# A two-layer hybrid decoder step on one core: inputs laid out on the host, a first stage by channel tiles, low weights and gate norms on VectorE, and new job ranks

## The chip, the cores and the metric

The kernel runs on one core of a Trainium2 chip as a single program. The metric is the device time of one execution in microseconds (us), as the median of several runs. PE is TensorE's matmul side and PEld its weight loads; DVE is VectorE, ACT ScalarE, POOL GpSimd, SP SyncE, from whose queue the kernel issues its DMAs.

## The reference

One inference step over a prompt of 1024 rows and 32 sample rows (8 sequences of 4), with 1024 channels and two layers. Each layer computes

```
x <- x + gate(c) * Branch(RMSNorm(x) * (1 + scale(c)) + shift(c)),   (shift, scale, gate) = silu(c) @ w_mod + b_mod
```

Layer 0 is sliding-window attention: 16 query heads on 4 key heads of 64 channels, a window of 128, a learned sink for each head, and for the samples a cache of 128 keys and values. Layer 1 is the gated DeltaNet: 8 query and key heads, 16 value heads of 128 channels, a causal convolution of length 4 ahead of q, k and v, and

```
S_t = e^{g_t} S_{t-1} + k_t u_t^T,   u_t = beta_t (v_t - (e^{g_t} S_{t-1})^T k_t),   o_t = S_t^T q_t / sqrt(128)
conv = silu(conv1d([conv_buf; h @ w_in][qkv]));   out = (rms_norm(o) * o_norm_g * silu(z)) @ w_out
```

The samples start from a state and a convolution buffer that are inputs. Outputs are y for both, the new keys and values, the new convolution buffers and the new states. Everything is float32.

## The kernel before, in words

All matrix products with weights are made of three products in a reduced form: both factors are split into a high and a low part (`wh`, `wl` for weights, `hhi`, `hlo` or `h2hi`, `h2lo` for activations), and high x high, high x low and low x high are summed in PSUM. The 1056 rows of both groups are handled as columns in three groups, `GRP`: 0 to 384, 384 to 768 and 768 to 1056. `project` takes, for one tile of 128 weight columns, 8 channel tiles x 3 products for each group, 72 products in all. `projector(plan)` runs a list of such tiles: `w_raw` loads raw weights two tiles ahead, and the job `ahead` splits the next tile's two halves when the counter `ticks`, one for each channel tile and group, has gone on by the two numbers of `SP`. `split_w` lets ACT cast the high part and POOL subtract it for the low part.

From the first attention projection on, the work around projections is written as generators. `weave(gen, name, hq)` puts one in a list of jobs by its rank (`K[name]`, or `KR[hq][name]` for a round's jobs), and after each product `stages()` goes through the list in order of rank and lets each job go on whose condition holds. The conditions (`ready`, `soon`, `idle`) look at engine-free times that the recording class `Core` adds up for each instruction as it is issued. So the ranks, `SP` and these times set one fixed order of instructions on each engine. Helpers issue through `Core`'s `Engine.call`, which is why nearly all instructions stand at one line of the kernel (L89).

The stages, with their times in the profiled execution:

- First stage, to 67 us. `scale_x` forms the row norms (twelve small DVE operations) and scales tiles of x in place; `turn_x` transposes them on PE, and ACT and DVE copy the results to `zo`. `modulation` multiplies silu(c) with halves of w_mod (products of 512 columns into one PSUM tile), `shape_h(0)` and `shape_h(1)` form hhi and hlo for four channel tiles each, and `first_half` makes the products for the first key and query tiles.
- Layer 0, to 415 us: the other projections, the attention of blocks, and `cached_pair`, which loads cached keys of two sequences and transposes them on PE. `modulation_rest` forms layer 1's modulation.
- The output projection of layer 0 and the shaping for layer 1, to 545 us.
- Layer 1, to about 1400 us: eight rounds, one for each key head, with six tiles of projection (q, k, two v, two z) as the stream between which jobs run. `conv` evacuates a projection into XR, convolves on DVE, and its job `samples` convolves the samples' columns on POOL with two PE transposes. `solve` and `invert` find the inverses of 64 triangular blocks of 32x32 on 64 partitions, by two DVE operations for each of 31 columns; `chain` runs through the eight chunks of 128 rows; `gating`, one job for each pair of chunks, norms the outputs (`rsqrt_pool`, on POOL) and multiplies with the gate.
- The output projection of layer 1 and the samples, to the end. `states_times` loads the samples' states and multiplies them with their keys and queries; `core` solves the samples' rule and updates the states.

Of the kernel before, what the change touches and what calls it, by code (L numbers as in the profile page):

```python
# [5 lines left out]
F32 = mybir.dt.float32  # L6
# [8 lines left out]
P = 128  # L15
# [16 lines left out]
def constants():  # L32
# [16 lines left out]
    blocks["lo32"] = (i[:, None] % 32 >= np.arange(32)[None, :]) * 1.0  # L49
# [9 lines left out]
    hsel = np.zeros((P, P))  # L59
    for kv in range(4):  # L60
        for r in range(32):
            hsel[kv * 4 + (r % 16) // 4, 32 * kv + r] = 1.0
    blocks["hsel"] = hsel
# [4 lines left out]
    order = ["ident", "iu", "ones", "mku", "lo32", "bsel", "fold32", "fold64", "wmask", "hsel", "smask", "selp", "sels"]  # L68
# [151 lines left out]
def body(tc, I, O, cst_ap, dbg=None):  # L220
    nc = tc.nc
    from contextlib import ExitStack, nullcontext
    es = ExitStack()
# [15 lines left out]
    SP = (2, 20)  # L239
    AM = (4, 8)  # L240
    K = dict(split=3, add=3, attend=12, turning=14, modulate=31, cached=9, wo=7, turn=0, ahead=6, taps=4, gating=5, decay=2, samples=28, load=5, mod=9, shape=9, decays=8, prepare=1, gather=11, finish=54, states=21, core=4, new=9)
    KR = [{'chain': 8, 'output': 9, 'solve': 5, 'invert': 21, 'blocks': 10, 'decayed': 0}, {'chain': 0, 'output': 3, 'solve': 12, 'invert': 10, 'blocks': 35, 'decayed': 35}, {'chain': 33, 'output': 2, 'solve': 22, 'invert': 19, 'blocks': 33, 'decayed': 34}, {'chain': 22, 'output': 12, 'solve': 3, 'invert': 4, 'blocks': 30, 'decayed': 17}, {'chain': 14, 'output': 0, 'solve': 1, 'invert': 17, 'blocks': 31, 'decayed': 57}, {'chain': 3, 'output': 13, 'solve': 6, 'invert': 20, 'blocks': 55, 'decayed': 29}, {'chain': 8, 'output': 1, 'solve': 11, 'invert': 20, 'blocks': 73, 'decayed': 34}, {'chain': 10, 'output': 8, 'solve': 4, 'invert': 28, 'blocks': 40, 'decayed': 44}]
# [10 lines left out]
    XB, FB, ZK, HK0, HK1 = 14, 3, 5, 7, 3  # L253
# [11 lines left out]
    gT = cp.tile([P, 2, KD], F32, name="gT")  # L265
    bT = cp.tile([P, 48], F32, name="bT")
# [9 lines left out]

    def xload(t):
        xt = xp.tile([P, D], F32, tag="xt", name="xt", bufs=XB)[0:P if t < NB else TS]
        nc.sync.dma_start(xt, xp_rows[t * P:(t + 1) * P] if t < NB else xs_rows)
        return xt  # L280

    def wmod_load(i):

        wms = []
        for k in range(KD):
# [2440 lines left out]
```

## Time and profile before

| | |
|---|---|
| time of the runs | 1695.62 us median of 3 (1692.66 to 1700.45) |
| profiled execution, span | 1699.2 us; the views give no other time for it |
| PE busy | 1613.3 us (95%) |
| PEld busy | 1417.4 us (83%) |
| DVE busy | 1207.9 us (71%) |
| ACT busy | 865.5 us (51%) |
| POOL busy | 581.8 us (34%) |
| granted clock, mean | 0.987 |
| DMA | 191.76 MB, 113 GB/s over the span |

A row of a table of stretches reads: stretch and length, busy time of each engine with the number of instructions, granted clock of PE, share of the DMA engines, GB/s. A row of a timeline reads: start, duration (of all its instructions), engine, line, operation, what it writes from what it reads, shapes, and in brackets the idle time ahead and who ended it. A group's row gives its busy time, the mean of one in ns, and the idle time ahead. A row of waits gives us in all, times and the longest.

### The profile page before, as it was taken

How to read it: one execution, taken by the hardware profiler on the slowest of the kernel's cores; microseconds unless marked ns; L12 is line 12 of the kernel's file. 1: busy time of each engine (PE TensorE's matmuls, PEld its weight loads, DVE VectorE, ACT ScalarE, POOL GpSimd, SP SyncE). 2: the span in 40 equal slices, each digit the busy share in tenths (PEclk: the TensorE clock that was granted, in tenths of full speed). 3: DMA queues.
4: the chain of work that ended last, by engine and by line, in shares of the span. 5: the costliest groups of instructions: out<-in, count | busy, mean ns of one | idle time of the engine just before them, and what ended most of it. 6: DMA issues, size and time to landing. Idle time of an engine off the chain costs nothing. (4 is left out here: it accounts for less than half of the span.)

```text
span 1699.2 us, 31431 instructions
## 1 busy us (share of the span) xinstructions
PE 1613.3 (95%) x10554; PEld 1417.4 (83%) x10554; DVE 1207.9 (71%) x3540; ACT 865.5 (51%) x2517; POOL 581.8 (34%) x1042
## 2 busy tenths in 40 slices
PE   6999999998999999999999999999999998989896
PEld 4988888986678899988989999899999996667784
DVE  5526676564665578878889788788788876367776
ACT  6625565443344565366463755655656654233332
POOL 2501111111222334363442644345344454333232
PEclk9999999998999999999999999999999999999998
DMA  9532121223343232132422324124241237855885
GB/s 345 158 123 73 53 59 48 59 81 93 116 136 105 79 77 65 59 99 73 118 56 69 89 66 129 46 79 111 54 124 49 55 97 225 245 165 169 243 259 166
DMA packets 281571, 191.76 MB, mean 113 GB/s; under 512 B 98361, under 2 KB 253881, under 8 KB 281378
## 3 DMA queue, kind: packets, MB, share of 16 engines
q1 hardware_dynamic: 281410, 189.75, 38.8%
q8 instruction: 84, 1.38, 0.4%
q14 instruction: 77, 0.63, 0.1%
HBM read 144.68 MB, written 47.04 MB: 113 GB/s over the span
## 5 line engine op out<-in xcount | busy, mean ns | idle before, releaser
L89 PE MATMUL ps_pj<-h2hi,wh 128*128 128x384 f32 (+1 forms) x1128 | 380.1, 337 | 0.0
L89 PE MATMUL ps_pj<-h2hi,wl 128*128 128x384 f32 (+1 forms) x1128 | 378.9, 336 | 0.6 <-POOL wl L89 0.5
L89 PE MATMUL ps_pj<-h2lo,wh 128*128 128x384 f32 (+1 forms) x1128 | 379.3, 336 | 0.0
L89 POOL TENSOR_TENSOR wl<-wr,wh 128x512 fp32r<-128x512 f32 x122 | 165.0, 1354 | 533.2 <-ACT wh L89 470.7
L89 PEld LDWEIGHTS ps_pj<-h2hi,wl 128*128 128x128 f32 x1128 | 213.5, 189 | 4.6 <-POOL wl L89 1.2
L89 PEld LDWEIGHTS ps_pj<-h2hi,wh 128*128 128x128 f32 x1128 | 213.5, 189 | 2.4
L89 PEld LDWEIGHTS ps_pj<-h2lo,wh 128*128 128x128 f32 x1128 | 213.2, 189 | 2.6
L89 POOL TENSOR_TENSOR xt<-xt,y 128x512 f32<-128x512 f32 (+1 forms) x48 | 63.6, 1329 | 174.3 <-DVE y L89 140.7
L89 PE MATMUL ps_pj<-hlo,wh 128*128 128x384 f32 (+1 forms) x360 | 119.6, 332 | 0.0
L89 PE MATMUL ps_pj<-hhi,wh 128*128 128x384 f32 (+1 forms) x360 | 119.0, 331 | 0.0
L89 PE MATMUL ps_pj<-hhi,wl 128*128 128x384 f32 (+1 forms) x360 | 118.7, 330 | 0.0
L89 DVE SCALAR_TENSOR_TENSOR vT<-XR,cT,vT 128x384 f32<-128x384 f32 (+1 forms) x144 | 91.8, 644 | 21.8 <-ACT vT L89 20.3
L89 DVE TENSOR_TENSOR X<-X,tmp 64x31 f32<-64x31 f32 (+15 forms) x248 | 94.5, 381 | 8.5
L89 DVE TENSOR_TENSOR tmp<-X 64x31 f32<-64x31 f32 (+15 forms) x248 | 95.9, 387 | 4.8 <-POOL X L89 1.5
L89 ACT CAST wh<-wr 128x512 fp32r<-128x512 f32 x122 | 75.1, 616 | 15.3 <-PE ps_pj L89 11.9
L89 PEld LDWEIGHTS ps_pj<-hlo,wh 128*128 128x128 f32 x360 | 68.2, 189 | 11.2 <-issue 11.1
L89 ACT COPY XR<-ps_pj 128x384 f32<-128x384 f32 (+1 forms) x96 | 43.2, 450 | 64.7 <-PE ps_pj L89 64.6
L89 PEld LDWEIGHTS ps_pj<-hhi,wh 128*128 128x128 f32 x360 | 68.3, 190 | 2.7 <-issue 2.7
L89 PEld LDWEIGHTS ps_pj<-hhi,wl 128*128 128x128 f32 x360 | 68.2, 189 | 2.1 <-issue 2.1
L89 ACT ACTIVATE prob<-prob,nm 128x256 f32<-128x256 f32 (+1 forms) x128 | 62.2, 489 | 14.9 <-DVE nm L89 14.7
L89 POOL TENSOR_TENSOR Xd<-Xc,cst 32x128 f32<-32x128 f32 x128 | 63.6, 497 | 16.1 <-DVE UZ L89 6.7
L89 ACT ACTIVATE qe<-ps_mi,Eg 128x128 f32<-128x128 f32 x112 | 35.0, 364 | 65.6 <-PE ps_mi L89 65.6
(575 smaller groups left out, 4177.2 us busy)
## 6 DMA issues: line engine op xcount, KB each, us to landing
wr<-in_gdn_w_in SPq DMA_DIRECT2D x96, 256.0 KB
S<-in_state_gdn_s SPq DMA_DIRECT2D x40, 256.0 KB
xt<-in_x_prompt SPq DMA_DIRECT2D x16, 512.0 KB
wm<-in_w_mod SPq DMA_DIRECT2D x16, 512.0 KB
wr<-in_swa_w_in SPq DMA_DIRECT2D x64, 128.0 KB
wmod<-in_w_mod SPq DMA_DIRECT2D x32, 256.0 KB
wm<-in_w_mod SPq DMA_DIRECT2D x32, 256.0 KB
DP<-gcr SPq DMA_DIRECT2D x64, 128.0 KB
```

Source lines behind the costliest of these rows:

```text
L89: inst = fn(*args, **kwargs)
```

## The change

- `relaid` lays inputs out by numpy on the host: w_mod by channel tile, weights by tiles of 128 columns, cached keys and small vectors transposed, the convolution buffer and the states by partition. Three outputs are written in layouts of their own and turned on the host. The PE transposes of small vectors, taps and cached keys go, and rows in DRAM become longer and contiguous.
- The first stage runs by channel tiles. `turn_x` transposes x unscaled, all 18 copies are DVE's; the norms' factors are spread to all partitions by small products (`spread_x`); `modulate(e)` and `fold` form shift and scale of one channel tile, `shape_h(k)` shapes it, and `first_part(k, p)` multiplies it at once. `queued` fixes SP's order.
- `w_halves`: the low weights of a projector are subtracted on DVE. `gating(g)` takes four chunks and norms them by `rsqrt` on DVE.
- The samples' convolution leaves the rounds: each `conv` writes its last 35 columns of XR to DRAM (`cvd`), and `samples(half)` in `states_times` convolves 16 tiles of 128 channels at once on DVE. `core` waits until both halves are convolved.
- `invert` runs on 128 partitions, even columns on the one half and odd ones on the other, with about half the elements for each operation. The loads of X and Xc double in number.
- New `SP`, `AM`, `K` and `KR` (two of their numbers are in the diff).

```diff
-    SP = (2, 20)
-    AM = (4, 8)
+    SP = (5, 21)
+    AM = (6, 9)
 ...
+        def w_halves(i, q):
+            hi, lo = (wq.tile([P, 4, P], F32R, tag=tag, name=tag, bufs=3) for tag in ("wh", "wl"))
+            nc.scalar.copy(hi, raws[i][q])
+            yield idle("vector", hi)
+            nc.vector.tensor_sub(lo, raws[i][q], f(hi))
+            halves_.setdefault(i, []).append((hi, lo))
 ...
-                        w_split(i + 1, q)
+                        yield from w_halves(i + 1, q)
 ...
+    def modulate(e):
+        pm = psb("mi")[:, 0:256]
+        for k in range(KD):
+            q = k % 4
+            nc.tensor.matmul(pm[32 * q:32 * q + 32, :], cT[:, k, :], wms[e, k // 4][:, q, :], start=(k < 4), stop=(k >= 4),
+                             skip_group_check=True)
 ...
+    def shape_h(k):
+        u = xp.tile([P, TP], F32, tag="fu", name="fu", bufs=FB)
+        sc, sh = Sc[0][:, k, 0:1], Sh[0][:, k, 0:1]
+        spans = [slice(0, GW), slice(GW, TP)]
+        for cs in spans:
+            nc.vector.scalar_tensor_tensor(u[:, cs], zo[k // 4][:, k % 4, cs], sc, rsb[:, cs], ALU.mult, ALU.mult)
+            nc.scalar.activation(hhi[:, k, cs], u[:, cs], AF.Identity, bias=sh)
+        for cs in spans:
+            nc.vector.scalar_tensor_tensor(hlo[:, k, cs], u[:, cs], sh, f(hhi[:, k, cs]), ALU.add, ALU.subtract)
 ...
+    for k in range(KD):
+        if k + 1 < KD:
+            fold(k + 1, ma)
+            shape_h(k + 1)
+        first_part(k, 0)
+        if k % 2 == 0 and k + 2 < KD:
+            fws[k // 2 + 1] = split_w(fraws.pop(k // 2 + 1))
+        first_part(k, 1)
+        if k + 2 < KD:
+            ma = modulate(k + 2)
+        if k + 4 < KD:
+            wmod_load(k + 4)
 ...
-            for r in range(2):
-                yield ready(kc)
-                pt = yield from bank("mi")
-                for kv in range(4):
-                    nc.tensor.transpose(pt[0:64, kv * P:(kv + 1) * P], kc[:, r, kv * 64:(kv + 1) * 64], ident)
 ...
-                    weave(samples(), "samples")
+                    nc.sync.dma_start(cvd[ct], XR[:, TP:TP + 35])
 ...
-                n, m = 31 - k, k + 1
+                n, m = 31 - k, k // 2 + 1
 ...
-                rsqrt_pool(nc, sm, fo, mo.rearrange("p h c -> p (h c)"), 4, "fo_")
+                rsqrt(nc, sm, fo, mo.rearrange("p a h c -> p (a h c)"), 8, tag="fo_")
 ...
+            raw, acc, tp = (wide(nm) for nm in ("raw", "acc", "tp"))
+            nc.sync.dma_start(raw, cvd[n0:n0 + 16, :, 3:35].rearrange("n p t -> p n t"))
+            nc.sync.dma_start(kept, I["keep"][half])
+            for i in range(DS):
+                dst = t4 if i else a4
+                for t0, src in ((0, k4[:, :, :, i:3]), (3 - i, x4[:, :, :, 0:i + 1])):
+                    nc.vector.tensor_tensor(dst[:, :, :, t0:t0 + n], src, taps.to_broadcast([P, 16, DB, n]), ALU.mult)
+                if i:
+                    nc.vector.tensor_tensor(acc, acc, tp, ALU.add)
 ...
+            qk = (yield from samples(0)).rearrange("p (i h) t -> p h i t", i=2)
+            yield from samples(1)
```

How this moves instructions shows best in their order. The first place is PE in the first stage. `ps_mi` is the modulation's PSUM tile, `cst` the constants (identity), `wm` pieces of w_mod, `ma` the modulation's sums; `ps_pj` and `ps_lg` hold the sums of the first products. Before, after the transposes of x:

```order
L650 MATMUL ps_ob<-cst,xt 128x32 x4
L344 MATMUL ps_mi<-wm_116,cT 32x512 x2
L344 MATMUL ps_mi<-wm_118,cT 32x512 x2
L344 MATMUL ps_mi<-wm_120,cT 32x512 x2
L344 MATMUL ps_mi<-wm_122,cT 32x512 x2
L344 MATMUL ps_mi<-wm_124,cT 32x512 x2
```

After, with `rsx` the norms' factors:

```order
L84 MATMUL ps_lg<-cst,rsx 128x128 x3
L84 MATMUL ps_mi<-wm_122,cT 32x256 x4
L84 MATMUL ps_mi<-wm_124,cT 32x256 x4
L84 MATMUL ps_ob<-cst,rsx 128x128 x3
L84 MATMUL ps_lg<-cst,rsx 128x128 x2
L84 MATMUL ps_lg<-cst,rsx 128x32
L84 MATMUL ps_mi<-cst,ma 128x32 x2
L84 MATMUL ps_mi<-wm_128,cT 32x256 x4
L84 MATMUL ps_mi<-wm_130,cT 32x256 x4
L84 MATMUL ps_mi<-cst,ma 128x32 x2
L84 MATMUL ps_pj<-hhi,wh 128x384
L84 MATMUL ps_pj<-hlo,wh 128x384
```

Eight products of 256 columns and two folds now stand ahead of the first projection product, where a whole half of the modulation, of 512 columns each, stood before.

The second place is the low weights in layer 1. On POOL before, `XS`, `us` and `tp` are the samples' columns, their sum and a tap's product:

```order
L89 TENSOR_TENSOR wl<-wr,wh 128x512 x2
L89 COPY XS<-XR_6021 128x8x4
L89 TENSOR_SCALAR us<-XS,cT 128x32
L89 TENSOR_SCALAR tp<-XS,cT 128x32
L89 TENSOR_TENSOR us<-us,tp 128x32
L89 TENSOR_SCALAR tp<-XS,cT 128x32
L89 TENSOR_TENSOR us<-us,tp 128x32
```

On DVE after, in the midst of an inversion (`X`, `tmp`) and a convolution (`kT`); `zl` is the gate's product:

```order
L84 SCALAR_TENSOR_TENSOR zl<-ps_tr,ong,zl 128x512
L84 SCALAR_TENSOR_TENSOR kT<-XR_6005,cT,kT 128x384
L84 TENSOR_TENSOR tmp<-X 128x120
L84 TENSOR_TENSOR X<-X,tmp 128x12x10
L84 TENSOR_TENSOR wl<-wr,wh 128x512
L84 SCALAR_TENSOR_TENSOR kT<-XR_6005,cT,kT 128x384
L84 TENSOR_TENSOR tmp<-X 128x121
L84 TENSOR_TENSOR X<-X,tmp 128x11x11
```

The subtraction has left POOL, which has no work of the samples there any more, and stands among the inversion's steps on DVE.

The third place is the end of PE's program. `ps_mi<-U,kb` is the last of the state updates, the others are the output projection. Before:

```order
L89 MATMUL ps_mi<-U_17746,kb 128x256
L89 MATMUL ps_pj<-whB_18508,ohi 64x512
L89 MATMUL ps_pj<-wlB_18509,ohi 64x512
L89 MATMUL ps_pj<-whB_18508,ohi 64x512
L89 MATMUL ps_pj<-wlB_18509,ohi 64x512
L89 MATMUL ps_pj<-whB_18508,ohi 64x512
```

After:

```order
L84 MATMUL ps_tr<-whB_17484,olo 128x512
L84 MATMUL ps_mi<-U_16678,kb 128x256
L84 MATMUL ps_tr<-wlB_17485,ohi 128x512
L84 MATMUL ps_tr<-h2hi,ohi 128x512
L84 MATMUL ps_tr<-h2hi,olo 128x512
L84 MATMUL ps_tr<-h2lo,ohi 128x512
```

Before, 62 products of the output projection follow the last state update; after, 22 do. The first product with a sample's state stands at number 7983 of 9031 before and 8042 of 8973 after.

606 lines of the change are left out of this document (272 added, 334 removed).

## The prediction

> **What bounds the kernel now.** I read the page first, for its head and its slices, then one table of stretches, then the timeline of the first 70 us, then the groups and the waits of the stretches that the change touches.
>
> ```profile
> span 1699.2 us, 31431 instructions
> PE 1613.3 (95%) x10554; PEld 1417.4 (83%) x10554; DVE 1207.9 (71%) x3540; ACT 865.5 (51%) x2517; POOL 581.8 (34%) x1042
> DMA  9532121223343232132422324124241237855885
> ```
>
> PE is busy for 95% of the span, so removed PE work counts nearly in full wherever PE has no idle time. The DMA row has two loaded places: the first slice and the last seven.
>
> ```profile
> 0.00:42.00 42.00, 25.40 (x150) 16.84 (x150) 23.90 (x75) 25.83 (x41) 11.24 (x17) 1.00 1.01 340
> 67.00:415.00 348.00, 336.91 (x2479) 295.09 (x2478) 199.63 (x720) 174.44 (x561) 50.41 (x42) 0.99 0.28 79
> 700.00:1000.00 300.00, 289.80 (x2072) 270.39 (x2071) 250.39 (x699) 175.63 (x552) 129.67 (x305) 1.00 0.30 80
> 1000.00:1300.00 300.00, 296.22 (x2116) 279.89 (x2115) 248.50 (x696) 172.88 (x544) 134.09 (x315) 1.00 0.31 84
> 1400.00:1500.00 100.00, 91.28 (x577) 64.65 (x571) 44.63 (x115) 36.59 (x106) 36.88 (x78) 0.97 0.80 233
> 1500.00:1600.00 100.00, 90.27 (x402) 70.47 (x401) 76.10 (x211) 37.45 (x76) 34.69 (x26) 0.95 0.61 187
> 1650.00:1700.00 50.00, 36.18 (x153) 26.57 (x151) 33.10 (x104) 11.92 (x29) 12.14 (x8) 0.90 0.54 166
> ```
>
> The columns are the stretch and its length, then busy time of PE, PEld, DVE, ACT and POOL, the granted clock, the DMA share and GB/s. Three kinds of stretch stand out. In the first 42 us PE is busy for 25.4, so this is a chain of arrivals and shaping. From 700 to 1300 PE has 14 idle us in 600, with DVE at 498.9 (83%). The last three rows have 8.7, 9.7 and 13.8 idle us of PE, the last of them mostly the closing norm and store, with DMA busy.
>
> **The first stage.** The timeline of before:
>
> ```profile
> 10.21 1.11 PE L650 MATMUL ps_pj<-cst,xt 128*128 128x128 f32 x4 [10.21 <-DVE xt L639]
> ...
> 16.14 1.11 PE L650 MATMUL ps_pj<-cst,xt 128*128 128x128 f32 x4 [3.96 <-DVE xt L639]
> ...
> 22.99 1.06 PE L650 MATMUL ps_lg<-cst,xt 128*128 128x128 f32 x4
> ...
> 28.09 0.68 DVE L659 COPY zo<-ps_ob 128x512 f32<-128x512 f32 x1
> ...
> 36.98 2.77 PE L344 MATMUL ps_mi<-wm,cT 128*32 128x512 f32 x20
> ...
> 39.68 0.44 PE L702 MATMUL ps_pj<-hhi,wh 128*128 128x384 f32 x1
> ...
> 66.68 0.34 PE L702 MATMUL ps_lg<-hhi,wl 128*128 128x384 f32 x1
> 66.86 0.29 PE L702 MATMUL ps_ob<-hhi,wh 128*128 128x288 f32 x1
> 66.99 0.29 PE L702 MATMUL ps_ob<-hlo,wh 128*128 128x288 f32 x1
> 67.12 0.30 PE L702 MATMUL ps_ob<-hhi,wl 128*128 128x288 f32 x1
> 67.26 0.33 PE L567 MATMUL ps_pj<-hhi,wh 128*128 128x384 f32 x1
> ```
>
> Before, the first transpose waits until 10.21 for x scaled on DVE, the second tile until 16.14, the first product starts at 39.68, and the next group of weights at 67.26. After, x is transposed unscaled. Its start is bounded by the landing of x: I take 5. Then 68 full transposes and 4 small ones follow; four of them cost about 0.85 (1.06 with their tail, in the row at 22.99), so 18 groups take 15.3; 18 DVE copies at 0.68 (row at 28.09) take 12.2 beside them, with one chain of twelve small operations for the norms between (12 x 0.17 by the row of mo below, 2.3 with gaps). That ends at 20.5. The other chain of the norms (2.3), the spread, one fold and the first shaped tile (before, from 36.98, where the fold has ended, to 39.68 is 2.7; with the spread I take 4) put the first product at 26 to 27.
>
> From there each of eight channel tiles costs PE 18 products: per head 3 x (0.174 + 0.174 + 0.131), by the steps between the rows 66.68, 66.86 and 66.99 (0.18 and 0.13), so 2.87 for two heads; eight modulation products of 256 columns, half of 8 x 2.77 / 20, so 0.55; and two folds, some 0.1. That is 3.5 us of PE a tile. The weights of one tile and its share of the product weights, 1.31 MB, at the 340 GB/s of the first row are 3.9 us, though loading starts long before. With 3.5 to 4.3 a tile the stage ends between 54 and 61; I take 59 against 67.26, **-8** (bounds -3 and -13). The far bound of a loss: if each tile waits fully for its own fold, copy and shaping, 2 us more a tile, the stage ends at 75, +8; the order excerpt speaks against it, since tile k+1 is folded and shaped while tile k multiplies.
>
> **Transposes that go.** In each of 32 convolutions of layer 1 PE transposes the samples' state and the samples' own columns; in layer 0 it transposes 32 tiles of cached keys.
>
> ```profile
> 1000.96 0.24 PE L89 MATMUL ps_tr<-cst,st 24*128 24x24 f32 x1
> 1001.12 0.30 PE L89 MATMUL ps_tr<-cst,XR 128*35 128x128 f32 x1
> 1001.18 0.42 PE L89 MATMUL ps_pj<-h2hi,wl 128*128 128x384 f32 x1
> ```
>
> ```profile
> 380.40 1.03 PE L89 MATMUL ps_mi<-cst,kc 128*64 128x128 f32 x8 [1.43 <-DMA kc<-in_cache_swa_k]
> 381.19 0.38 PE L89 MATMUL ps_pj<-hhi,wh 128*128 128x288 f32 x1
> ```
>
> From 1000.96 to 1001.18 a pair takes 0.22; 32 pairs are 7.0. Leaving and entering the stream of products costs up to 0.12 more, so the bounds are -7 and -11; I take **-8**. Eight keys take 0.79 (380.40 to 381.19), so 32 take 3.2, and the wait of 1.43 ahead goes as well: **-4.5** (-3 to -5). Both lie where PE has next to no idle time, in the rows of 67 to 415 and 700 to 1300, so nothing hides them.
>
> **Work that changes engine in layer 1.** The terms are in these rows (busy time, mean ns of one):
>
> ```profile
> L89 POOL TENSOR_TENSOR wl<-wr,wh 128x512 fp32r<-128x512 f32 x122 | 165.0, 1354 | 533.2 <-ACT wh L89 470.7 <-PE ps_lg L89 24.5 <-ACT XS L89 10.1
> L89 DVE TENSOR_TENSOR olo<-zo,ohi 128x512 fp32r<-128x512 f32 x16 | 11.5, 726 | 3.1 <-ACT ohi L89 3.0
> L89 DVE TENSOR_TENSOR tmp<-X 64x256 f32<-64x256 f32 x8 | 3.3, 418 | 0.1
> L89 DVE TENSOR_TENSOR tmp<-X 64x31 f32<-64x31 f32 x16 | 3.0, 185 | 1.7 <-POOL X L89 1.5
> L89 DVE SCALAR_TENSOR_TENSOR mo<-mo,epq 128x4 f32<-128x4 f32 x32 | 5.4, 170 | 5.3 <-ACT jc L89 5.2
> L675 DVE TENSOR_TENSOR hlo<-fu,hhi 128x1024 fp32r<-128x1024 f32 x2 | 5.9, 2973 | 0.7 <-ACT hhi L674 0.7
> ```
>
> The low weights of 47 projections, 94 subtractions of 128x512, come to DVE. The same operation there takes 0.726 (olo), so +68 us of DVE, against 127 off POOL. The gate norms add about 128 DVE operations of 0.17, +22. The inversions lose half their columns: over one inversion the products of rows and columns fall from 5456 elements to 2856, for two operations each and eight inversions 41,600 elements; 418 - 185 ns over 225 elements is 1.04 ns, so -43. DVE ends up with 46 us more over the 855 us of layer 1, 32 of it in the 600 us of the two rows: 531 of 600, 88%. What hides this is the stream of products: PE waits for DVE only where DVE comes late, which the next rows price.
>
> The waits of PE between 545 and 1400, and between 1400 and 1700:
>
> ```profile
> PE ps_tr L89 <- ACT vT L89: 7.2, 5, 2.5
> PE ps_mi L89 <- DVE us L89: 3.6, 4, 1.3
> PE ps_pj L89 <- POOL wl L89: 0.5, 1, 0.5
> ```
>
> ```profile
> PE ps_mi L89 <- ACT kb L89: 6.6, 4, 3.4
> PE ps_lg L89 <- DVE KQT L89: 4.0, 1, 4.0
> PE ps_lg L89 <- DMA S<-in_state_gdn_s: 2.3, 3, 1.9
> ```
>
> All waits for the low weights are 0.5 us now. The chain of the rounds, which waits for us on DVE, held PE up for 3.6 us in 855. ACT's 7.2 for vT should shrink, as ACT loses 96 small operations of the samples and DVE its clashes with POOL. I take **-2** for this part (-6 to +33). The 33 would be 47 projections that each wait 0.7 us, one DVE operation that stands ahead of the low weights. Queued behind the low weights on DVE are then the convolutions' sums and the inversion's steps, for which solve and chain wait.
>
> [...] The row at L675 shows DVE at 2.97 us for 1024 elements a partition while POOL did the same subtraction; two operations of 0.726, from the row of olo, would be 1.45. So one clash cost 1.5 us. [...] By rows: with no clash the added DVE work is 46; with a clash in a quarter of the 94 subtractions, had POOL stayed loaded, it would be 46 + 24 x 1.5 = 82. POOL is nearly empty in layer 1 after the change, so I take 46.
>
> **The samples' convolution at the end.** It becomes 20 DVE operations of 128x512, 20 x 0.726 = 14.5 us, after the last projection and ahead of the samples' state products. DVE is busy for 44.6 of 100 us from 1400 to 1500, and PE there has the second half of the output projection to do, so most is hidden; the samples' chain starts 8 to 15 us later. On the DMA queue of SP some seven transfers more stand ahead of the state loads, against 160 that leave the rounds:
>
> ```profile
> L89 SPq DMA_DIRECT2D out_new_conv_s<-cvo x96: 625/632/1222, 569.5 to 1383.0; - x96
> ```
>
> At 0.63 an issue the seven are 4.4 us; the inversions' 40 more loads, 25 us over eight rounds, take the room of the 96 that go, 61. State loads and stores run in longer pieces, which answers to the 2.3 us that PE waits for S. I take **0** (-8 to +12). What is late if the cover goes: the waits for kb and KQT, 10.6 us now.
>
> **New ranks.** They set which waiting step goes first; the trace of before has no price for them. The waits listed here sum to 24; half of them either way, -12 to +12, is the bound, and I take **0**.
>
> **Sum.** -8 - 8 - 4.5 - 2 = -22.5. The views give the profiled execution's span, 1699.2, which is 3.6 over the median of the runs, 1695.62; against its own span the sum gives 1676.7, and against the median, to which the result is compared, **1673**.
>
> **Rivals.** *DVE becomes the bound in layer 1.* The second half of the next projection's weights is cut at step 21 of 24 (SP) and first used four steps into that projection. A step is three products, some 0.48 us, so 7 steps leave 3.3 us for ACT's cast and DVE's 0.73; two or three operations ahead of it on DVE use that up, while DVE is busy for 88%. For it speaks that DVE is the busiest engine after PE; against it, that the same margin held for POOL at 1.35 each (8 steps, 3.8 us, with 0.5 us of waits in all). It decides, against the -22.5 below, once PE waits over 0.5 us in each of the 47 projections. At 0.7 each, one operation, it is 33: 1673 + 33 = 1706. Chance 0.10. [...]
>
> *The tail gives back.* The samples' chain starts 15 us later, and products of the output projection that covered it run out, so that the idle time of 1500 to 1700 grows by 15: 1688. Chance 0.10.
>
> *More goes than counted.* The first stage runs at its 3.5 us a tile (-13), the transposes cost 11, state transfers and ranks give 6 and 4 more in the tail: -40, 1655. For it speaks the idle time in the first and last rows; against it, that each is a bound. Chance 0.25.
>
> **How the numbers follow.** The forecast case has 0.55, from 1663 to 1685. The lower rival spreads from there to 1640, most of it above 1647, and the tail rival to 1697. Leaving out the DVE rival and what lies below, the range is 1647 to 1697. A measurement of this kernel tells about 0.5% from no change, 8.5 us: faster means under 1687.1, slower over 1704.1. Faster: 0.55 + 0.25 + 0.04 = 0.84; same 0.07, slower 0.09.
>
> **What would show it.** Right: the first projection with one set of weights for all columns starts near 59; in layer 1 no ps_tr from st or XR; DVE near 88% with PE idle not over 14 in 600 us. Wrong: PE waits for wl on DVE of over 10 us in sum, a first stage that ends after 64, or over 40 idle us of PE after 1400 (counted back from the end).

## The result and the profile after

The changed kernel takes 1698.69 us (median; 1695.43 to 1706.71), the kernel before beside it 1696.9. The ratio is 1.0011, with a 95% interval from 0.9994 to 1.0028: no change that can be told, where 1673 with a range from 1647 to 1697 was forecast. The head of the page and the loaded slices of DMA:

```profile
span 1696.6 us, 30465 instructions
PE 1602.7 (94%) x10544; PEld 1419.6 (84%) x10544; DVE 1218.4 (72%) x3797; ACT 845.1 (50%) x2414; POOL 237.6 (14%) x321
DMA  9332211125242323133313224232242156773785
```

PE lost 10.6 us of work, so work did go; the idle time grew by 8. POOL has given up 344 us for 10.5 more on DVE. The table of stretches, same columns as before:

```profile
0.00:42.00 42.00, 30.16 (x179) 25.26 (x180) 23.82 (x58) 18.54 (x33) 10.95 (x26) 0.84 0.93 350
700.00:1000.00 300.00, 284.34 (x2010) 269.10 (x2009) 245.92 (x774) 171.71 (x525) 27.50 (x57) 0.97 0.30 85
1000.00:1300.00 300.00, 292.56 (x2092) 279.27 (x2091) 244.98 (x772) 173.93 (x528) 27.17 (x54) 0.99 0.31 88
1400.00:1500.00 100.00, 85.78 (x431) 58.31 (x432) 48.08 (x120) 30.44 (x88) 23.12 (x24) 0.93 0.74 212
1500.00:1600.00 100.00, 85.13 (x368) 64.51 (x367) 73.75 (x195) 37.25 (x75) 32.27 (x23) 0.91 0.56 177
1650.00:1700.00 50.00, 35.10 (x160) 27.00 (x158) 35.59 (x111) 12.81 (x31) 10.26 (x8) 0.91 0.50 166
```

From 700 to 1300 PE now idles 23 us, not 14, while DVE has fallen to 490.9 of 600 (82%, forecast 88%). From 1400 to 1600 PE idles 29 us, 18 before, and the granted clock there is lower, 0.93 and 0.91 for 0.97 and 0.95.

Where the time went, by the starts of the same instructions in the two timelines (us; a profile of other kernels below moved such a mark by up to 4 us where nothing ahead of it had changed, so smaller differences say little):

| stretch ends with | before | after | change in the stretch | forecast |
|---|---|---|---|---|
| first projection with one set of weights | 67.26 | 75.00 | +7.7 | -8 |
| first product of layer 0's output projection | 417.32 | 412.89 | -12.2 | -4.5 |
| first projection of layer 1 | 551.40 | 544.20 | -2.8 | 0 |
| last projection of layer 1 | 1413.09 | 1395.30 | -10.6 | -10 |
| last product on PE | 1688.86 | 1685.10 | +14.0 | 0 |
| end of the span | 1699.21 | 1696.62 | +1.2 | 0 |

Two stretches, the first stage and the tail, miss by 30 us together. The timeline of the first stage after, on PE:

```profile
24.96 1.22 PE L84 MATMUL ps_ob<-cst,rsx 128*128 128x128 f32 x4 [2.81 <-DVE rsx L84]
...
27.53 1.06 PE L84 MATMUL ps_mi<-cst,ma 128*128 128x32 f32 x4
28.52 1.94 PE L84 MATMUL ps_mi<-wm,cT 128*32 128x256 f32 x16
31.75 1.06 PE L84 MATMUL ps_mi<-cst,ma 128*128 128x32 f32 x4 [1.29 <-ACT ma L84]
32.62 0.67 PE L84 MATMUL ps_pj<-hhi,wh 128*128 128x384 f32 x1
...
40.16 0.42 PE L84 MATMUL ps_pj<-hhi,wh 128*128 128x384 f32 x1
...
43.25 1.07 PE L84 MATMUL ps_mi<-wm,cT 128*32 128x256 f32 x16
44.87 0.63 PE L84 MATMUL ps_mi<-cst,ma 128*128 128x32 f32 x4 [0.55 <-ACT ma L84]
45.34 0.42 PE L84 MATMUL ps_pj<-hhi,wh 128*128 128x384 f32 x1
...
75.00 0.41 PE L537 MATMUL ps_pj<-hhi,wh 128*128 128x384 f32 x1 [2.67 <-DVE kll L806]
```

The first product starts at 32.62, not 26 to 27, and the first channel tile takes 7.54 us, most of it at half the clock (0.50 granted; see the last section). From 40.16 a tile takes 5.18 us: its 18 products 3.09, its share of the modulation 1.07, a wait of 0.55 for ACT's copy `ma`, and the fold 0.47. A last wait of 2.67 follows, as the two heads end together and their sums are still to be taken out of PSUM.

PE's waits in layer 1 (545 to 1400), then in the tail (1400 to 1700):

```profile
PE ps_tr L84 <- DVE zl L84: 9.6, 5, 4.3
PE ps_mi L84 <- DVE us L84: 3.3, 4, 2.2
PE ps_tr L84 <- ACT vT L84: 1.6, 3, 0.8
PE ps_pj L84 <- DVE wl L84: 0.9, 1, 0.9
```

```profile
PE ps_lg L84 <- DMA S<-in_states: 8.2, 5, 3.3
PE ps_mi L84 <- ACT kb L84: 7.9, 5, 2.1
PE ps_mi L84 <- DVE us L84: 6.7, 3, 3.9
```

The low weights cost 0.9 on DVE. The waits for vT have fallen from 7.2 to 1.6, but a new one stands first: the gate's product `zl`, 9.6. In the tail the wait for the samples' states has grown from 2.3 to 8.2.

### The profile page after: what moved, and what is told of

It is laid out like the page before. It is cut to its first block, busy times and chain, and to the rows that moved or that the text cites. A ratio compares the mean times of both kernels' runs of the same rounds, so it can differ in the third digit from the quotient of the medians.

```text
span 1696.6 us, 30465 instructions
## 1 busy us (share of the span) xinstructions
PE 1602.7 (94%) x10544; PEld 1419.6 (84%) x10544; DVE 1218.4 (72%) x3797; ACT 845.1 (50%) x2414; POOL 237.6 (14%) x321
## 4 chain that ended last, share of the span: by engine, by line
PE 43%; DVE 9%; DMA 9%; ACT 3%; issue 2%; SPq 1%; POOL 0%; POOLq 0%; DVEq 0%; ACTq 0%
PE ps_pj L84 27%; PE ps_lg L84 6%; PE ps_mi L84 5%; PE ps_ob L84 2%; PE ps_tr L84 2%; DMA gTd<-zl 2%; DMA S<-in_states 1%; DMA zl<-zd 1%; DMA of<-gTd 1%; DMA out_new_s_s<-S 1%; DVE zl L84 1%; DMA wr<-in_gdn_w_out 1%; DMA out_y_p<-xt 1%; DVE S L84 1%; DVE rst L84 1%
## 5 line engine op out<-in xcount | busy, mean ns | idle before, releaser
L84 POOL TENSOR_TENSOR Xd<-Xc,cst 32x128 f32<-32x128 f32 x128 | 68.5, 535 | 435.0 <-DMA Xc<-Xdd 251.5
L84 PE MATMUL ps_pj<-hlo,wh 128*128 128x384 f32 (+1 forms) x376 | 124.7, 332 | 0.0
L84 PE MATMUL ps_pj<-hhi,wh 128*128 128x384 f32 (+1 forms) x376 | 124.7, 332 | 0.0
L84 PE MATMUL ps_pj<-hhi,wl 128*128 128x384 f32 (+1 forms) x376 | 123.6, 329 | 0.0
L84 DVE TENSOR_TENSOR wl<-wr,wh 128x512 fp32r<-128x512 f32 x120 | 83.3, 694 | 15.5 <-ACT wh L84 15.1
L84 DVE SCALAR_TENSOR_TENSOR vT<-XR,cT,vT 128x384 f32<-128x384 f32 (+1 forms) x144 | 80.8, 572 | 9.9 <-ACT vT L84 9.2
L84 ACT CAST wh<-wr 128x512 fp32r<-128x512 f32 x128 | 78.6, 616 | 16.9 <-PE ps_pj L84 15.2
L84 PEld LDWEIGHTS ps_pj<-hlo,wh 128*128 128x128 f32 x376 | 71.0, 189 | 10.6 <-issue 10.2
L84 DVE TENSOR_TENSOR X<-X,tmp 128x126 f32<-128x126 f32 (+22 forms) x248 | 63.8, 257 | 8.5
L84 DVE TENSOR_TENSOR tmp<-X 128x126 f32<-128x126 f32 (+22 forms) x248 | 62.3, 251 | 7.3 <-POOL X L84 3.4
```

Source lines behind the costliest of these rows:

```text
L84: inst = fn(*args, **kwargs)
```

## Experiments

Ratios are to the kernel before (1695 to 1697 us in every group of runs), with 95% intervals; the changed kernel's is 1.0011. Theory A says that each repaired wait or removed work is time; theory B, that the fixed order takes it back later.

### The first stage

**e1_early_mod** issues the modulation of tile k+2 between the two heads' products, so that ACT's copy is hidden by nine products:

```diff
+        if k + 2 < KD:
+            ma = modulate(k + 2)
 ...
         first_part(k, 1)
-        if k + 2 < KD:
-            ma = modulate(k + 2)
```

> The changed kernel with one move: in the first stage the modulation products of tile k+2 are issued between the two heads' products of tile k instead of behind them. Theory A (PE waits in each tile for ACT's copy of the modulation's sums, 0.92 us a tile, because fold(k+2) follows right behind them): the 4.6 us of waits for ma in the first stage go, a tile takes 4.2 instead of 5.17, the stage ends near 68 to 69 instead of 75.0, and the time falls by 5 to 7 us against the changed kernel. Theory B (each tile is limited by DVE's and ACT's shaping, 3.2 us of DVE a tile in a chain with the products): a wait for hhi or hlo takes the place of the one for ma and the stage ends at 73 or later, time the same within 2 us.

1695.62 us, ratio 0.9998 (0.9986 to 1.0011). The waits for `ma` up to 76 us fall from 4.6 to one:

```profile
PE ps_mi L84 <- ACT ma L84: 1.3, 1, 1.3
```

The stage ends at 71.63, 3.4 us earlier, and the kernel gains 3.1. So A holds, at half the size expected: the modulation's products and the fold themselves stay on PE.

**e8_old_first** puts the old first stage back into the changed kernel (`modulation`, `scale_x`, `turn_x` and `shape_h` as before; all else as changed).

> The changed kernel with the first stage of the kernel before put back (x scaled before it is transposed, two halves of the modulation, products after each half); all else as changed. Theory A (the stage by channel tiles ends 7.7 us later than the old one, and layer 0 carries that on): the next projection starts at 67 in place of 75.0 and the time falls by 6 to 9 us against the changed kernel, to a ratio near 0.996 to the kernel before. Theory B (what the first stage loses is taken up later, since layer 0 and the tail are paced by other things): under 3 us.

1704.49 us, ratio 1.0043 (1.0026 to 1.0061): slower, though the stage ends at 70.88, 4.1 us earlier (the same stage ended at 67.26 before, so not all of the 7.7 us is the new stage's own). In layer 1 PE's rows stand in the same order as in the changed kernel, and yet its last projection starts 5 us later. The waits from 545 to 1400 have no new kind, only a little more of several (of the changed kernel: zl 9.6, gss 2.3):

```profile
PE ps_tr L84 <- DVE zl L84: 9.3, 5, 4.4
PE ps_lg L84 <- DVE gss L84: 3.5, 1, 3.5
```

A, that the new first stage costs its whole difference, fell here: of the 4.1 us, 2.2 are gone by the start of layer 1, and 7.1 are lost in it, in small pieces whose trigger the trace doesn't name.

### The gate's product

**e2_zl2** gives zl two buffers and issues both loads of a gating job at its start:

```diff
-    ZB, VB, SB = 1, 3, 4
+    ZB, VB, SB = 2, 3, 4
...
+                for cp_ in (2 * g, 2 * g + 1):
+                    zls.append(gp.tile([P, 2, 2 * P], F32, tag="zl", name="zl", bufs=ZB))
+                    nc.sync.dma_start(zls[-1], ...)
 ...
-                    zl = gp.tile([P, 2, 2 * P], F32, tag="zl", name="zl", bufs=ZB)
+                    zl = zls[a]
 ...
-                    nc.sync.dma_start(zl, ...)
```

> The changed kernel with two buffers for zl in place of one, and both loads of a gating job issued ahead of its norm chain. Theory A (in layer 1 DVE waits for the second load of zl, which is issued only after the first block was stored, and PE then waits 9.6 us in sum for the bank that DVE frees late): PE's waits for DVE zl fall from 9.6 to under 2 us, and the time falls by 5 to 10 us. Theory B (VectorE as such is the bound of layer 1, with 46 us more work): other waits for DVE (us, S, vT) take their place and the time stays within 2 us.

1691.87 us, ratio 0.9971 (0.9958 to 0.9984), 6.8 us better than the changed kernel. The waits for zl in layer 1:

```profile
PE ps_tr L84 <- DVE zl L84: 1.9, 3, 1.3
```

The last projection starts 26.9 us earlier. Of these, 16 are no gain: the order formed anew, and 134 products of the rounds' chains that stood ahead of the last projection now stand behind it. PE's idle time within layer 1 fell by 11 us (24.9 to 13.5), and the end of PE's program keeps 5.6 of them; where the rest went shows below. As to the cause in the changed kernel, A holds: its gating job takes four chunks but holds one buffer, so the second load waits until the first block is stored, and DVE waits for these loads nine times, 14.8 us in all. What the new order adds to the 6.8 us can't be told apart. **e11_old_first_zl2** joins the last two edits.

> The old first stage and the two zl buffers together on the changed kernel. Theory A (first stage and zl waits are separate losses that add): 6 to 9 and 6.8 us, together 12 to 16 us less than the changed kernel, ratio to the kernel before 0.991 to 0.994. Theory B (the tail takes up what comes early, as it took 21 us of the 27 that the zl buffers had won by the last projection): not over 8 us less.

1692.38 us, ratio 0.9976 (0.996 to 0.9992): the 5.8 us that the old first stage cost alone are down to 0.5 (against e2). The two don't add, as B says.

### The samples' convolution and its place

**e3_no_conv** leaves out its 20 DVE operations, their buffers and the load of the kept rows; the load of the columns, the silu and the store stay.

```diff
-            raw, acc, tp = (wide(nm) for nm in ("raw", "acc", "tp"))
+            raw = acc = wide("raw")
-            for i in range(DS):
 ...
```

> The changed kernel without the samples' convolution at the end: the 20 DVE operations and the loads of the kept rows are left out, the raw rows go through the activation only. Theory A (the convolution delays the first product with a sample's state to 1445, 50 us behind the last projection, and holds the buffers of the states): that product moves to about 1425, waits for S of 8.2 us fall under 4, and the time falls by 6 to 12 us. Theory B (the tail is paced by the positions of the output projection, which the samples' chain only has to keep up with): the product moves but the time changes by under 3 us.

1689.91 us, ratio 0.9958 (0.9944 to 0.9972), 9 us. In the changed kernel the convolution runs on DVE, among other jobs, from the first to the last of these operations:

```profile
1409.06 0.55 DVE L84 TENSOR_TENSOR acc<-kept,cT 128x384 f32<-128x384 f32 x1
...
1440.52 0.69 DVE L84 TENSOR_TENSOR acc<-acc,tp 128x512 f32<-128x512 f32 x1
```

Without it the first product with a state starts at 1419.72 and not at 1445.19, and PE's wait for the states is back under its value of before:

```profile
PE ps_lg L84 <- DMA S<-in_states: 1.4, 2, 1.0
```

**e6_tail** keeps the convolution, with scratch in other buffers so that the states can load beside it, and its second half as a job of its own.

```diff
-            yield from samples(1)
-            for _ in range(SB):
-                fetch()
+            weave(samples(1), "samples")
 ...
+            for _ in range(SB):
+                fetch()
```

> The changed kernel with the whole convolution kept, but in buffers of its own: the states' loads start ahead of it, and its second half is a job beside the state products instead of ahead of them. Theory A (as in the run without convolution): the waits for S fall from 8.2 to under 4 us and the time falls by 4 to 10 us, near what leaving the convolution out gives. Theory B (paced by the output projection): within 2 us. If the run without the convolution gains and this one does not, the DVE work itself is the price and not the buffers.

1704.83 us, ratio 1.0054 (1.0041 to 1.0068), 6 us slower than the changed kernel. The first state product came 7.7 us earlier, but the silu of the second half came 3.1 us later, and `core` waits for both halves:

```profile
PE ps_mi L84 <- ACT kb L84: 10.6, 4, 6.8
PE ps_lg L84 <- DMA qk<-smd: 4.1, 1, 4.1
```

The waits for the states only fell from 8.2 to 6.2 us. So nothing here speaks for the buffers as the cause; as the run moves the second half too, it doesn't rule out a share of theirs.

### Low weights, their engine and the table of ranks

**e4_wl_pool** issues the low weights of the projectors on GpSimd again, and lets the order form anew. These are 120 subtractions, 28 of them ahead of layer 1.

```diff
-                        yield from w_halves(i + 1, q)
+                        w_split(i + 1, q)
```

> The changed kernel with the low weights of the projectors on GpSimd again, as before; ranks and all else as changed. Theory A (the low weights on VectorE cost nothing in layer 1, since PE waits for them 0.9 us in all): the time stays within 4 us, up or down, the order of all jobs being shifted too. Theory B (VectorE with 83 us more of subtractions is what eats the gain): the time falls by 8 us or more, waits for DVE in layer 1 go down from 21 us in sum to under 10.

1731.38 us, ratio 1.021 (1.0181 to 1.0239): 33 us slower than the changed kernel, which neither theory had. **e12_wl_pool_same** does the same, with the times that the order is made from left as they are for VectorE (in `w_halves`; `moved` issues on the second engine and counts on the first):

```diff
-            nc.vector.tensor_sub(lo, raws[i][q], f(hi))
+            nc.moved("vector", "gpsimd", "tensor_sub", lo, raws[i][q], f(hi))
```

> The changed kernel with the 120 subtractions wl of layer 1 issued on GpSimd again, while TensorE's and ScalarE's rows stay in exactly the order of the changed kernel (GpSimd gains 120 x about 1.35 us, VectorE loses 120 x 694 ns = 83 us). Theory C, the move to VectorE itself is worth little and what the earlier GpSimd run lost (1731) came from the order that was made anew around it: within 6 us of the changed kernel's 1698.7, waits of TensorE for wl under 3 us. Theory D, the engine is what counts, since GpSimd's long operations slow VectorE's copies beside them: vT's mean goes back from about 572 to about 640 ns, TensorE waits over 5 us for vT in layer 1, and the time is 1706 to 1716.

1720.77 us, ratio 1.0144 (1.0124 to 1.0163). **e13_wl_dve_before** is the reverse: the kernel before, PE's order kept, with those subtractions on VectorE (`nc.moved("gpsimd", "vector", ...)` in `projected`'s splits).

> The kernel before with only the 120 subtractions wl of layer 1 issued on VectorE, TensorE's and ScalarE's rows in exactly the order of before. Prediction's own term: about -2 us, with bounds -6 to +33. Theory C: within 6 us of before's 1696.9, waits for wl up to 5 us in all. Theory D: vT's mean falls from 644 to about 580 ns and TensorE's 7.2 us of waits for vT with it, so 5 to 9 us faster, 1688 to 1692. The rival of the prediction, VectorE becomes the bound: more than 10 us of waits for wl or us, and 1703 or more.

1701.5 us, ratio 1.0023 (1.0009 to 1.0038). The convolution's sums in the groups of e12 and then of e13:

```profile
L84 DVE SCALAR_TENSOR_TENSOR vT<-XR,cT,vT 128x384 f32<-128x384 f32 (+1 forms) x144 | 89.9, 636 | 12.9 <-ACT vT L84 12.1
```

```profile
L89 DVE SCALAR_TENSOR_TENSOR vT<-XR,cT,vT 128x384 f32<-128x384 f32 (+1 forms) x144 | 80.9, 567 | 17.3 <-ACT vT L89 16.0
```

With GpSimd loaded a sum takes 636 ns, without 567 (644 before, 572 in the changed kernel), so DVE's sums are slower beside a loaded GpSimd. Yet in the order of before the faster sums bring nothing, and in the order after GpSimd's load costs 22 us. PE doesn't wait for the low weights there; it waits for DVE's S and us, 6.8 and 6.0 us (2.5 and 3.3 in the changed kernel). Theory D is half right: the engine counts, in the order fitted to it.

**e5_old_ranks** is the changed kernel with the whole old table, **e17_old_sp_am** with only `SP` and `AM` of before, **e15_before_new_ranks** the kernel before with the new table.

```diff
-    SP = (5, 21)
-    AM = (6, 9)
+    SP = (2, 20)
+    AM = (4, 8)
```

> The changed kernel with the ranks and the two pairs of numbers (SP, AM) of the kernel before. Theory A (the new ranks are what gave layer 0 its 12 us, by taking the cached pairs and the last attention earlier: before, 10 us lay between the last projection product and the first output product, after 0.1): the first output product comes 5 us or more later than in the changed kernel, and the time rises by 4 to 12 us. Theory B (layer 0 gained by the cached keys and VectorE free of clashes alone): the first output product within 3 us of the changed kernel's 412.9.

> The changed kernel with SP and AM of before (when the next weights are cut, when the shaping comes), K and KR as changed. If the table's 96 us hang on the time at which the low weights are cut, for which VectorE now stands in GpSimd's place, most of them come back here: 1760 or more, with waits for wl of over 10 us. If they hang on the ranks of the rounds' jobs (K, KR), this stays under 1725, with waits for wl under 5 us.

> The kernel before with only the table of ranks (SP, AM, K, KR) of the changed kernel. If the new ranks are better as such, it is faster than before, by 5 to 15 us. If each table is fitted to the operations of its own kernel, as the 96 us suggest that the old table cost the changed kernel, it is 30 to 100 us slower, mostly in layer 1, with waits for vT, us and wl of over 10 us in all. The prediction's term for the ranks was 0 with bounds of 12 us to either side.

1792.68 us, ratio 1.0559 (1.0532 to 1.0587); 1743.88 us, 1.0289 (1.0256 to 1.0323); 1735.72 us, 1.0221 (1.0195 to 1.0247). e5 is 94 us slower than the changed kernel, far outside the 4 to 12 that were expected. Long waits of e5 in layer 1, then the longest of e17:

```profile
PE ps_tr L84 <- ACT vT L84: 27.0, 13, 14.4
...
PE ps_pj L84 <- DVE wl L84: 11.7, 7, 3.0
```

```profile
PE ps_pj L84 <- DVE wl L84: 8.9, 3, 4.1
```

Each kernel is 39 to 94 us faster with its own table than with the other's. SP and AM alone, which set when the next weights are cut and how far ahead of PE a step may be issued, make 45 of the 94; e17 fell between its two cases. In e15 the first product of the output projection starts 9.2 us earlier than before: in layer 0 the new table is a gain by itself, and in layer 1, where it loses 30, it is not. The changed kernel says the same: its stretch of layer 0 takes 337.9 us, 345.7 with the old table (e5), and the kernel before takes 350.1, or 348.0 in e16, which changes nothing there. So 8 us of the gain in layer 0 are the table's, and 2 to 4 are left for the cached keys and the other edits.

### The transposes

**e16_no_turn** takes the 64 transposes of the samples' columns out of the kernel before, with everything else in the same order.

```diff
-                        nc.tensor.transpose(pt[:, 0:24], st, ident[0:24, 0:24])
-                        nc.tensor.transpose(pt[0:35, P:2 * P], XR[:, TP:TP + 35], ident)
 ...
```

The two copies of their results, on ACT, read XR instead.

> The kernel before without the 64 transposes of the samples' columns in layer 1 (their results, so the samples' outputs and the new convolution buffers, aren't the reference's); every other instruction stands in the same order on every engine. If PE's time is what ends layer 1, as the prediction had it, the 32 pairs give 7 to 11 us: 1686 to 1690, and the last projection of layer 1 starts 7 to 11 us earlier. If a fixed order takes back what is cut out of PE, by waits of PE for vT and us that come earlier with it, under 4 us are left: 1693 or more.

1686.36 us, ratio 0.9951 (0.9933 to 0.9969), so 8.3 us (5.3 to 11.4). The forecast's -8 was right: taken out of a fitted order, PE's work is time, as theory A has it. The marks of the one profile are coarser: layer 1 is 5.9 us shorter, with 3.8 us gained ahead of it, where nothing had changed.

### The repairs together, and the end of the tail

**e14_best** joins e1, e2 and a third edit (in `turn_x`, the last norms of x are formed ahead of the last tile's copies). **e18_best_noconv** is e14 without the convolution, as in e3.

```diff
+        nc.scalar.activation(sq[0:parts], xts[t], AF.Square, accum_out=xss[0:parts, n:n + 1])
+        if n == NB:
+            scale_x(5, 9)
         for kk in range(2):
 ...
-        nc.scalar.activation(sq[0:parts], xts[t], AF.Square, accum_out=xss[0:parts, n:n + 1])
 ...
-    scale_x(5, 9)
```

> The changed kernel with three edits: the modulation of tile k+2 between the two heads' products of tile k, two buffers for zl with both loads ahead, and the scaling of the last four x tiles' norms ahead of the last tile's copies in the first stage. Theory A, each repaired wait is time: -3.1 (the first edit alone) -6.8 (the second alone) -2 to -3 (the third, the 2.8 us wait for rsx), so 1685 to 1688. Theory B, what comes before the tail is soaked up by the tail and by a lower granted clock behind each new gap: no better than the second edit alone, 1690 to 1694.

> The three repairs of e14 and, as in e3, the samples' convolution left out (the samples' outputs aren't the reference's). If the losses add up: 1686.9 - 9 = 1678. If the tail has a floor of its own by the states' loads and the chain of updates, and the repairs before it and this one pull at the same idle time: 1682 or more.

1686.85 us, ratio 0.9938 (0.9919 to 0.9957), and 1664.4 us, ratio 0.9814 (0.9782 to 0.9845). The repairs add up, though the third isn't shown by itself: it wasn't run alone, and in e14 PE waits 3.77 us at its place, for DVE's `zo`, where it waited 2.81 for the norms. In e18 the convolution seems worth 22 us and not 9. The last state update and the last product of the changed kernel, of e14 and of e18, in the timeline of PE:

```profile
1679.74 0.28 PE L84 MATMUL ps_mi<-U,kb 96*128 96x256 f32 x1
...
1684.71 0.39 PE L84 MATMUL ps_ob<-h2lo,ohi 128*128 128x512 f32 x1
```

```profile
1648.67 0.28 PE L84 MATMUL ps_mi<-U,kb 96*128 96x256 f32 x1
...
1669.17 0.39 PE L84 MATMUL ps_ob<-h2lo,ohi 128*128 128x512 f32 x1
```

```profile
1649.09 0.39 PE L84 MATMUL ps_ob<-h2lo,ohi 128*128 128x512 f32 x1
```

Behind the update PE works on for 5.4 us in the changed kernel and for 20.9 in e14 and e2; in e18, whose last update starts at 1644.13, for 5.4. In PE's order these are 22, 89 and 22 products of the output projection (62 before): with new times the order had put the cover behind the updates instead of between them. Three runs change only the tail's order of e14: **e19_best_sw0** and **e20_best_sw3** its pacing `SW`, **e21_best_states0** the rank of the states' job.

```diff
-    SW = (1, 16)
+    SW = (0, 16)    # e19; (3, 16) in e20
 ...
-    'states': 21
+    'states': 0     # e21
```

> As e14, with the pacing of the samples' state products SW = (0, 16) in place of (1, 16); on PE few rows move up to the last state product, and 22 products follow the last update of a state instead of 89. If the loss of the tail is this cover in the wrong place (89 - 22 = 67 products of 512 columns, some 15 us after the last update): 1670 to 1676. If it is the convolution's own chain ahead of the first state product, which stays: 1683 to 1688 as e14.

> As e14, with SW = (3, 16): the state products are paced two steps later, and again 22 products follow the last update. By the order of the end: 1670 to 1678. By the convolution's chain, or because the later state products push the chain of updates back: 1683 or more.

> As e14, with the rank of the states' job (K, states) 0 in place of 21, so that the samples' convolution goes first where several jobs can go on; 22 products follow the last update. By the order of the end: 1670 to 1676, and if the convolution's place in the queue counts too, the first state product starts up to 10 us earlier than in e14 and the time goes to 1660 to 1670.

The count of 22 in these expectations holds for e21 alone; in the programs that ran, 89 follow the last update in e19 and 45 in e20.

| kernel | products behind the last update | us behind it | PE idle from the last projection to that update | time | ratio |
|---|---|---|---|---|---|
| e14 | 89 | 20.9 | 41.2 | 1686.85 | 0.9938 |
| e19 | 89 | 20.9 | 40.3 | 1690.9 | 0.9965 (0.9945 to 0.9984) |
| e20 | 45 | 10.7 | 30.8 | 1676.4 | 0.9874 (0.9853 to 0.9895) |
| e21 | 22 | 5.4 | 29.5 | 1673.23 | 0.9856 (0.9833 to 0.9879) |
| e18 (no convolution) | 22 | 5.4 | 25.4 | 1664.4 | 0.9814 |

All five have the same PE work behind the last projection. A product behind the update takes 0.24 us; one that moves ahead of it fills idle time there, as the fourth column shows. The time follows the count, though not product by product: from 89 to 45 it falls by 10 to 15 us (44 products are 10.3), from 45 to 22 by 3.2 (5.4), and e14 and e19 lie 4 us apart at one count. e19, which kept the count, gained nothing, against its forecast. At the same count, e18 against e21, the convolution is worth 8.8 us by the times and 7.1 by the ratios, near the 9 of e3. e21 beats both kernels, by 1.4% and 1.5%.

## Why the prediction was wrong

**The first stage: the term of -8 was mis-sized by 16.** The far bound, an end at 75, is what came, but not by waits for shaping. The step that failed first is the price of eight modulation products: the row at 36.98 counts two records a product, which the x16 of the rows at 28.52 and 43.25 for eight products shows, so the price was 1.07, not 0.55. The second is the order excerpt: tile k+1 is indeed shaped under tile k's products, but the next fold stands right behind its own modulation, with ACT's copy between them; 0.55 of wait and 0.47 of fold stood at "some 0.1" (e1 shows the wait's part). With 3.09 for the products these make 5.18, not 3.5 to 4.3. The third is the start, 32.62 for 26 to 27: a 2.81 wait for the norms, a second fold and a second modulation ahead of the first product, and half the clock (0.50 granted from 25 to 35, 0.71 from 35 to 40), with which the first tile takes 7.54. The wait of 2.67 at the end had no term. Two counts of the prediction are slips beside this: x has 64 full transposes and 8 small ones, in the same 18 groups, and by the kernel's shapes a tile's weights are 1.18 MB, not 1.31.

**The transposes** were right (e16). Of the cached keys no run takes out the change alone: layer 0 gained 12.2 where 4.5 was forecast, but with the old table (e5) 2 to 4, give or take the 4 us of such a mark, and the rest is the table's.

**Work that changes engine** came out near its sum (layer 1: -10.6 for -10) for partly other reasons. Low weights wait 0.9, vT 1.6, so the rival in which DVE becomes the bound is refuted. DVE's share stayed below the forecast for three reasons: the inversions gave back 64 us of DVE and not 43, the gate norms took 12 and not 22, and the sums of the convolutions became 16 us shorter in all (those into vT by 11%). But the step priced only the operations of `gating` and not its one buffer: 9.6 us of waits, 6.8 of time (e2).

**The samples at the end, 0, was the second mis-sized term.** It came out at +14. The convolution costs 9 us of this (e3; 7 to 9 by e18 against e21): the rival of the tail, with a chance of 0.10, had the right mechanism, and that its 15 lies so near 14 is partly luck. The prediction took the convolution's 14.5 us of DVE work as mostly hidden, since DVE had room. The work was only 12.0 us, but the chain stretched: its ten operations of a half stand among other jobs, and in the changed kernel both halves take from 1409 to 1441. No experiment accounts for the other 5; the granted clock from 1400 to 1600 (0.97 and 0.95 before, 0.93 and 0.91 after) goes with them, as cause or as effect.

**The ranks, 0 with 12 to either side**, failed as a term. The table without the rest of the change costs 39 us, the rest without the table 96 (1792.68 for 1696.9). They are not a part that can be added; bounds from the waits of before say nothing about an order that is made anew.

**The sum:** the six stretches miss by +15.7, -7.7, -2.8, -0.6, +14.0 and +1.2, together 19.8 of the 22.5. The rival of more gains, at 0.25, needed a first stage at 3.5 us a tile. Two of the three signs of being wrong that the prediction named came: a first stage that ends after 64 (75.00), and over 40 idle us of PE after 1400 (42.6, counted back from the end); the waits for wl did not. That e21 takes 1673 us, the very number forecast, is luck: its first stage ends at 70.85, not 59, and the convolution still costs its 9 us.

## What to carry over

Where a program's order is made from estimated times, price a change together with its order: what is left between the last dependent step and the end (here 0.24 us a product) can cost as much as the work taken out has gained. When a producer, a copy on another engine and a consumer follow one another on a full engine, put other products between them (nine in e1), and when a job takes two blocks instead of one, ask for its second buffer. In a trace, settle how many records one instruction leaves before a duration is divided by a count.

## What the hardware showed

The granted clock of PE in stretches of 5 us of the changed kernel (the second value from the right is the DMA share, the one ahead of it the clock):

```profile
20.00:25.00 5.00, 1.73 (x21) 0.76 (x20) 4.53 (x15) 1.37 (x3) 1.26 (x1) 0.92 1.04 405
25.00:30.00 5.00, 5.00 (x30) 3.76 (x30) 1.31 (x4) 1.06 (x3) 1.60 (x5) 0.50 1.03 408
30.00:35.00 5.00, 3.71 (x20) 3.25 (x13) 4.14 (x8) 2.43 (x5) 2.70 (x6) 0.50 1.02 404
35.00:40.00 5.00, 4.45 (x31) 3.63 (x30) 1.08 (x2) 1.41 (x3) 1.78 (x2) 0.71 0.96 366
...
75.00:80.00 5.00, 5.00 (x20) 5.00 (x21) 4.34 (x9) 4.87 (x11) 3.40 (x3) 0.66 0.99 356
```

Within the idle 2.81 us ahead of 24.96 the clock falls to half, and what the first four rows lack to full speed makes 13.7 us at half; products of 384 columns step by 0.32 us and not 0.174. After the wait of 2.67 ahead of 75.00 it is half again, for 3.4 us. So gaps of 2.81 and 2.67 us on PE went with a fall to half here. Before, the clock is full (1.00) from 27.5 to the end of the first stage. Ahead of the first gap the transposes sped up in the changed kernel:

```profile
12.73 1.06 PE L84 MATMUL ps_lg<-cst,xt 128*128 128x128 f32 x4
13.59 0.80 PE L84 MATMUL ps_tr<-cst,xt 128*128 128x128 f32 x4
14.22 0.60 PE L84 MATMUL ps_ob<-cst,xt 128*128 128x128 f32 x4
14.66 0.60 PE L84 MATMUL ps_pj<-cst,xt 128*128 128x128 f32 x4
```

Four of them step by 0.86 us up to 13.59 and by 0.44 from 14.22. The views print a clock of 1.00 on both sides of this, but the trace holds no clock at all ahead of 14.0 us (27.5 in the kernel before), so that figure says nothing there. In e16 the same step of the transposes falls where the clock is known; its rows, and the clock from 20 to 22.5 and from 23 to 26:

```profile
21.96 0.60 PE L664 MATMUL ps_lg<-cst,xt 128*128 128x128 f32 x4
22.40 0.76 PE L664 MATMUL ps_pj<-cst,xt 128*128 128x128 f32 x4
22.96 1.06 PE L664 MATMUL ps_lg<-cst,xt 128*128 128x128 f32 x4
23.81 1.06 PE L664 MATMUL ps_ob<-cst,xt 128*128 128x128 f32 x4
```

```profile
20.00:22.50 2.50, 1.36 (x13) 1.24 (x12) 2.24 (x6) 1.91 (x2) 0.00 (x0) 1.00 1.05 387
23.00:26.00 3.00, 3.00 (x11) 1.65 (x9) 2.58 (x15) 1.21 (x3) 0.00 (x0) 0.50 1.04 379
```

At a granted 1.00 four transposes step by 0.44 there, at 0.50 by 0.85. So, by its step, the 0.85 from which the prediction priced them was the price at half the clock. In the changed kernel PE had run nothing but transposes up to 14.22, from where they step by 0.44; so here transposes alone led up to full speed.
